# A decoder block on one core: the mixers' steps cut at each hand-over with TensorE, weight splits ordered two blocks ahead, and gv, gr as 512-column blocks

## The chip, the core and the metric

The kernel runs on one core of a Trainium2 chip, as one launch. The metric is the device time of a run in microseconds. The engines are TensorE (PE; its weight loads are PEld), VectorE (DVE), ScalarE (ACT), GpSimd (POOL) and SyncE (SP), whose queue issues the DMAs.

## The reference, cut to what matters

One block over 2048 positions of width 1024, in fp32:

```python
mod = (silu(c) @ w_ada + b_ada)                    # shift, scale, gate for each half
h = rms_norm(x, norm1_g) * (1 + sc1) + sh1
gq, gk, gv, gr, glr, aq, ak, av = split(h @ w_in)  # 256, 256, 512, 512, 16, 512, 512, 512 columns
log_a = log_sigmoid(glr @ gla_w_gate + gla_b_gate) / 16
y_gla = rms_norm(gated_linear_attention(gq, gk, gv, log_a)) * silu(gr)    # 4 heads
y_att = dilated_attention(rms_norm(aq), rms_norm(ak), av)   # 8 heads, windows (128,1), (512,4), (2048,16), merged by their denominators
x = x + g1 * (concat(y_gla, y_att) @ w_out)
h = rms_norm(x, norm2_g) * (1 + sc2) + sh2
u_gate, u_val = split(causal_conv3(h @ w_up))      # 2 x 2816 columns
x = x + g2 * ((silu(u_gate) * u_val) @ w_down)
```

## The kernel before, in words

The 2048 positions go in four chunks c of T = 512. Each large product is three fp32r matmuls for every 128 rows k of the inner dimension (mm3, L233): both operands are split into a high part (hi, rounded to fp32r) and the rest (lo), and hi x hi, hi x lo and lo x hi are added up in one accumulator bank. Weights come as blocks of 512 KB: a DMA into wraw (2 buffers), a cast on ScalarE to whi (L223) and a subtraction on VectorE, or POOL, to wlo (L224), 3 buffers each (wslot, L214). Large products use 4 accumulator banks (psg, given by pg()), the small ones 4 others (psa).

The stages of a chunk:

- proj(c) multiplies the normalised chunk by w_in. Channel blocks (chan: q, k of the attention with their norm, gq, gk) have the weights as stationary operand and 512 positions as columns. Token blocks (tok(b), L393; b = 0, 1 is gv, 2, 3 gr, 4, 5 av; b = 0 holds the 16 columns of glr too) have 128 positions as stationary operand and 256 (272) weight columns. Their results go to DRAM (gv, rg, v and so on). In tok(3) a hook makes the next chunk's normalised pieces hhi, hlo (norm_mod1, L327): eight pieces, one for each k, in 9 buffers.
- mix(c) is the mixer: gla (L465) for two halves of the chunk, then attn (L592) for four pairs of heads. gla makes scores at eight levels (VectorE, ScalarE exponentials, POOL product kh at L525, 32-wide matmuls at L500), then the output and the state. attn makes the scores of three branches (L651 for the 16-dilated one, scores() at L631 for the others) with a running maximum mx, exponentials (soft, L641) with their sums dn, a merging of the branches' denominators in which two small matmuls move values across partitions (with constants x1 at L685 and x4 at L703), scaling by the weights f, transposes (turn, L722) and the products with v (L746, L751). Their results y go to DRAM.
- outproj(c) loads y, splits it and multiplies by w_out; then follow a second norm and ffn(c) with down().

All of these are Python generators; a yield ends a step. beside(a, na, b, nb) takes a step of b and then na/nb steps of a, so the products of one chunk (b) are issued among the mixer steps of another (a): mix(0) beside proj(1) to proj(3), mix(1) beside outproj(0) and ffn(0), and so on. The framework then schedules: each instruction's place in the code is its priority, and on a simulated timeline every engine takes the first that is ready. What comes out is a fixed order for each engine, which the chip follows strictly.

Of the kernel before, what the change touches and what calls it, by code (L numbers as in the profile page):

```python
# [27 lines left out]
FIRST = (0, 1, 2, 3)  # L28

# [99 lines left out]
class K:  # L129
# [102 lines left out]

    def mm3(self, ps, ws, hs, first=True, shared=False):  # L233

        nc = self.nc
        n = len(ws)
        for k in range(n):
            (wh, wl), (hh, hl) = ws[k], hs[k]
            nc.tensor.matmul(ps, wh, hh, start=first and k == 0, stop=False, skip_group_check=shared)  # L239
            nc.tensor.matmul(ps, wh, hl, start=False, stop=False, skip_group_check=shared)  # L240
            nc.tensor.matmul(ps, wl, hh, start=False, stop=k == n - 1, skip_group_check=shared)  # L241
# [97 lines left out]
    def proj(self, c, hs, hook=None, done=()):  # L339
# [45 lines left out]
        def glaqk(b):  # L385
            ps = done[b] if b in done else chan(A["w_ch"][b])
# [6 lines left out]
        def tok(b):  # L393
            if b == 0:
                w = self.wblock(A["w_tok0"][0], 4, 272) + self.wblock(A["w_tok0"][1], 4, 272)
            else:
                w = self.wblock(A["w_tok"][b - 1, 0], 4, 256) + self.wblock(A["w_tok"][b - 1, 1], 4, 256)
            pss = []
# [8 lines left out]
            if b == 3 and hook:  # L407
                hook()
            for s2 in range(2):
                st = stage()  # L410
                if b:
                    ps = pss[s2]
                for s in range(2 if b == 0 else 0):
                    ps = self.pg()
                    tk = slice((2 * s2 + s) * P, (2 * s2 + s + 1) * P)
                    self.mm3(ps[:, 0:272], [(h[:, tk], l[:, tk]) for h, l in hs], w)
                    nc.scalar.copy(st[:, s * 256:(s + 1) * 256], ps[:, 0:256])
                    nc.scalar.copy(gl[:, 2 * s2 + s], ps[:, 256:272])
                v = lambda t: t.rearrange("p (s n) -> p s n", s=2)
                if b // 2 == 1:  # L420
                    nc.scalar.activation(st, ps, AF.Tanh, scale=0.5)
                    nc.vector.scalar_tensor_tensor(st, st, 1.0, ps, op0=ALU.add, op1=ALU.mult)  # L422
# [17 lines left out]
        if done:  # L440
            yield from chain(glaqk(0), glaqk(1), glaqk(2), glaqk(3), tok(0), qk(0), qk(1), tok(1), qk(2), qk(3), tok(4), qk(4), tok(5), qk(5), qk(6), tok(2), qk(7), tok(3))
        else:
            yield from chain(tok(0), qk(0), qk(1), tok(1), qk(2), glaqk(0), qk(3), tok(4), qk(4), glaqk(1), qk(5), tok(5), qk(6), glaqk(2), qk(7), tok(2), glaqk(3), tok(3))
# [21 lines left out]
    def gla(self, c, a):  # L465
# [47 lines left out]
        scores(gk, gq, 0)  # L513
        yield
        for s in (32, 16, 8, 4, 2, 1, 64):
# [10 lines left out]
            scores(kh, qh, s)  # L526
            yield
# [9 lines left out]
        nc.gpsimd.tensor_tensor(el, gk, el, op=ALU.mult)  # L537
        ps = self.pa()
# [8 lines left out]
        for s in range(2):  # L547
            sb = self.sb[s]
            part = lambda t, j: t[j:j + 32].rearrange("p e (h s) q -> p e h s q", s=2)[:, :, :, s]
            full = lambda j, q: sb[j:j + 32, :, q:q + 32].rearrange("p (h e) q -> p e h q", e=2)  # L550
            for j in range(0, P, 32):
                nc.vector.tensor_copy(full(j, j), part(av, j))
            for j in (0, 64):
                nc.gpsimd.tensor_copy(full(j, j + 32), part(a32, j))
            for e in range(2):
                nc.scalar.copy(sb[0:64, e::2, 64:P], off[e][0:64, 0:256].rearrange("p (h s q) -> p h s q", h=2, s=2)[:, :, s])
# [20 lines left out]
        nc.scalar.activation(ss, ss, AF.Exp, scale=-0.5)  # L577
        for s in range(2):
            o = os[s]
            y = t2("pt", 5)  # L580
            for hd in range(4):
                nc.vector.scalar_tensor_tensor(y[:, hd * P:(hd + 1) * P], o[:, hd * P:(hd + 1) * P], ss[:, s, hd:hd + 1], rg[:, s * T + hd * P:s * T + (hd + 1) * P], op0=ALU.mult, op1=ALU.mult)
            ps = self.pa()
            for hd in range(4):
                nc.tensor.transpose(ps[:, hd * P:(hd + 1) * P], y[:, hd * P:(hd + 1) * P], self.C("id"))
# [3 lines left out]
            yield  # L589


    def attn(self, c, hp):  # L592
# [22 lines left out]
        S = []  # L615
# [28 lines left out]
        slp = self.C("slp")[:, 24 * hp:24 * hp + 24].rearrange("p (a g i) -> p a g i", a=2, g=3)  # L644
        for hh in range(2):
# [19 lines left out]
        yield  # L665
# [3 lines left out]
        for hh in range(2):  # L669
            nc.vector.scalar_tensor_tensor(nm[:, hh], mx[:, hh], -1.0, slp[:, hh], op0=ALU.mult, op1=ALU.mult)  # L670
# [12 lines left out]
        nc.vector.tensor_tensor(xm, mv[:, :, None, :].to_broadcast(x4), self.C("s1")[:, None, :, None].to_broadcast(x4), op=ALU.mult)  # L683
        ps = self.pa()
# [16 lines left out]
        nc.vector.tensor_tensor(xm, f[:, :, 2][:, :, None, :].to_broadcast(x2), self.C("s4")[:, None, :, None].to_broadcast(x2), op=ALU.mult)  # L701
        ps = self.pa()
# [4 lines left out]
        yield  # L707
        for hh in range(2):
            _, s4, sn = S[hh]
            for i in range(4):  # L710
                z = 0 if c else P
                nc.vector.tensor_scalar(s4[:, i, z:], s4[:, i, z:], f[:, hh, 1, i:i + 1], None, op0=ALU.mult)
# [279 lines left out]
```

## Time and profile before

| | |
|---|---|
| median of 3 runs | 2737.36 us (2737.02 to 2742.2) |
| the profiled execution | 2739.4 us, span 2737.6 us |
| granted TensorE clock, mean | 0.978 |
| DMA packets moved | 405.19 MB, 148 GB/s |
| span | TensorE busy 96%, VectorE 69%, ScalarE 46%, POOL 19% |

The page gives for each engine its busy time, share of the span and instructions. Matmuls overlap in the pipeline, so the time that one adds is read from start to start of neighbours and not from its duration. "Granted clock" is the share of full speed at which TensorE was allowed to run. In a row of waits, `PE psa L685 <- DVE xm L683` is a matmul of line 685 that waited for VectorE's line 683.

### The profile page before, as it was taken

The numbers are of one execution on the slowest core, as the hardware profiler recorded it, in microseconds if no ns is written. First come the engines' busy times: TensorE is split into PE (matmuls) and PEld (weight loads), VectorE is DVE, ScalarE is ACT, GpSimd is POOL, SyncE is SP. The second block draws the span as 40 slices with busy tenths as digits, with TensorE's granted clock in tenths as the row PEclk, the third lists the DMA queues.
The fourth block names the chain that finished last, engine by engine and source line by source line (L and its number), as shares of the span: only waits on it lengthen the run. The fifth ranks groups of instructions, "written<-read, shape, count | busy, mean of one in ns | idle before, by whom it ended". The sixth has DMA issues, their size and how long they took to land.

```text
span 2737.6 us, 48297 instructions
## 1 busy us (share of the span) xinstructions
PE 2622.8 (96%) x18920; PEld 2172.7 (79%) x18920; DVE 1889.6 (69%) x3740; ACT 1265.5 (46%) x2606; POOL 518.8 (19%) x324
## 2 busy tenths in 40 slices
PE   5989999999979999999999999999999999999999
PEld 4978888888858887778777888887777788788887
DVE  8777575555567776667987677778877667575655
ACT  3555456465435444443544444435444444343332
POOL 1233242222222211100230111013111100011110
PEclk9999999999979999999999999999999999999999
DMA  7877454554632333336434444544443435333232
GB/s 276 289 260 243 145 186 154 195 173 147 197 113 93 99 123 122 106 122 232 137 97 124 130 136 126 169 168 128 130 129 113 140 122 187 125 100 100 93 100 93
DMA packets 196230, 405.19 MB, mean 148 GB/s; under 512 B 19474, under 2 KB 78627, under 8 KB 194723
## 3 DMA queue, kind: packets, MB, share of 16 engines
q1 hardware_dynamic: 196002, 402.11, 45.1%
q8 instruction: 149, 2.44, 0.4%
q14 instruction: 79, 0.64, 0.1%
HBM read 339.12 MB, written 62.91 MB: 147 GB/s over the span
## 4 chain that ended last, share of the span: by engine, by line
PE 66%; DVE 14%; ACT 9%; DMA 7%; issue 3%; SPq 1%; POOL 0%; DVEq 0%; ACTq 0%; POOLq 0%
PE psg L239 19%; PE psg L241 19%; PE psg L240 19%; DMA wada<-in_w_ada_dram 3%; ACT big L641 3%; DVE wlo L224 2%; PE psa L722 2%; PE psa L631 2%; PE psa L751 2%; ACT whi L223 1%; ACT s L641 1%; DVE big L637 1%; DMA sq<-in_xT_dram 1%; DVE wada L281 1%; DVE y L819 1%
## 5 line engine op out<-in xcount | busy, mean ns | idle before, releaser
L239 PE MATMUL psg<-hhi,whi 128*128 128x512 f32 x2040 | 818.5, 403 | 21.9 <-ACT hhi L333 10.4
L241 PE MATMUL psg<-hhi,wlo 128*128 128x512 f32 x2040 | 808.8, 397 | 10.6 <-DVE wlo L224 10.5
L240 PE MATMUL psg<-hlo,whi 128*128 128x512 f32 x2040 | 808.4, 397 | 7.2 <-DVE hlo L335 7.1
L223 ACT CAST whi<-wraw 128x1024 fp32r<-128x1024 f32 x391 | 408.6, 1049 | 573.9 <-PE psg L240 400.5
L224 DVE TENSOR_TENSOR wlo<-wraw,whi 128x1024 fp32r<-128x1024 f32 (+1 forms) x300 | 393.8, 1313 | 188.4 <-ACT whi L223 177.1
L224 POOL TENSOR_TENSOR wlo<-wraw,whi 128x1024 fp32r<-128x1024 f32 x91 | 225.6, 2479 | 1392.7 <-ACT whi L223 1169.3
L239 PEld LDWEIGHTS psg<-hhi,whi 128*128 128x128 f32 x2040 | 390.1, 191 | 115.9 <-ACT hhi L333 13.9
L241 PEld LDWEIGHTS psg<-hhi,wlo 128*128 128x128 f32 x2040 | 389.4, 191 | 96.2 <-DVE wlo L224 13.9
L240 PEld LDWEIGHTS psg<-hlo,whi 128*128 128x128 f32 x2040 | 390.3, 191 | 89.5 <-DVE hlo L335 10.8
L239 PE MATMUL psg<-ghi,whi 128*128 128x512 f32 x704 | 279.3, 397 | 0.0
L240 PE MATMUL psg<-glo,whi 128*128 128x512 f32 x704 | 277.1, 394 | 0.0
L241 PE MATMUL psg<-ghi,wlo 128*128 128x512 f32 x704 | 274.4, 391 | 0.0
L863 DVE SCALAR_TENSOR_TENSOR x<-psg,mod,x 128x512 f32<-128x512 f32 x192 | 143.0, 748 | 159.2 <-PE psg L241 154.8
L239 PE MATMUL psg<-whi,hhi 128*128 128x256 f32 (+1 forms) x768 | 222.5, 292 | 7.9 <-DVE stg L422 3.9
L241 PE MATMUL psg<-whi,hlo 128*128 128x256 f32 (+1 forms) x768 | 222.1, 292 | 5.6 <-DVE hlo L335 5.6
L240 PE MATMUL psg<-wlo,hhi 128*128 128x256 f32 (+1 forms) x768 | 221.4, 290 | 0.4 <-DVE wlo L224 0.4
L819 DVE SCALAR_TENSOR_TENSOR y<-psg,conv_w_sb,y 128x511 f32<-128x511 f32 x176 | 130.9, 744 | 94.1 <-ACT y L818 93.5
L239 PEld LDWEIGHTS psg<-whi,hhi 128*128 128x128 f32 x768 | 149.8, 196 | 12.4 <-issue 3.7
L239 PEld LDWEIGHTS psg<-ghi,whi 128*128 128x128 f32 x704 | 132.2, 188 | 33.1 <-issue 5.4
L241 PEld LDWEIGHTS psg<-whi,hlo 128*128 128x128 f32 x768 | 149.8, 196 | 8.5 <-DVE hlo L335 6.8
L240 PEld LDWEIGHTS psg<-glo,whi 128*128 128x128 f32 x704 | 132.3, 188 | 28.8 <-issue 3.1
L241 PEld LDWEIGHTS psg<-ghi,wlo 128*128 128x128 f32 x704 | 132.2, 188 | 27.9 <-DVE wlo L224 0.6
(198 smaller groups left out, 3672.9 us busy)
## 6 DMA issues: line engine op xcount, KB each, us to landing
wraw<-in_w_up_dram SPq DMA_DIRECT2D x176, 512.0 KB, 3.4
wraw<-in_w_down_dram SPq DMA_DIRECT2D x88, 512.0 KB, 3.4
wraw<-in_w_ch_dram SPq DMA_DIRECT2D x48, 512.0 KB, 4.0
wada<-in_w_ada_dram SPq DMA_DIRECT2D x40, 512.0 KB, 5.0
wraw<-in_w_tok_dram SPq DMA_DIRECT2D x40, 512.0 KB, 4.0
v<-v SPq DMA_DIRECT2D x68, 256.0 KB, 5.1
wraw<-in_w_out_dram SPq DMA_DIRECT2D x32, 512.0 KB, 4.0
sq<-in_xT_dram SPq DMA_DIRECT2D x48, 256.0 KB, 3.7
```

The source lines that it names most:

```text
L223: nc.scalar.copy(hi[:, :n], raw[:, :n])
L224: (nc.gpsimd if pool else nc.vector).tensor_tensor(lo[:, :n], raw[:, :n], hi[:, :n].bitcast(F32), op=ALU.subtract)
L239: nc.tensor.matmul(ps, wh, hh, start=first and k == 0, stop=False, skip_group_check=shared)
L240: nc.tensor.matmul(ps, wh, hl, start=False, stop=False, skip_group_check=shared)
L241: nc.tensor.matmul(ps, wl, hh, start=False, stop=k == n - 1, skip_group_check=shared)
L281: self.last = nc.vector.tensor_tensor_reduce(raw, raw, self.cond[:, i * n:(i + 1) * n], 0.5, m if i else 0.0, ALU.mult, ALU.add, m)
L631: nc.tensor.matmul(at(i, hh, z), q[H[hh], i * P:(i + 1) * P], key(H[hh], i, z), start=True, stop=True, skip_group_check=True)
L641: nc.scalar.activation(t[:, lo:hi], t[:, lo:hi], AF.Exp, bias=nm[:, hh, g, i:i + 1], scale=2.0 ** -(h + 1), accum_out=dn[:, hh, g, i:i + 1])
L722: nc.tensor.transpose(ps[:n, i * P:(i + 1) * P], part(S[hh], i), self.C("id"))
L751: nc.tensor.matmul(out, lhsT, rhs, start=first[hh], stop=False, skip_group_check=True)
L819: nc.vector.scalar_tensor_tensor(y[:, 1:], ps[:, :T - 1], self.cw[:, 1, b:b + 1], y[:, 1:], op0=ALU.mult, op1=ALU.add)
L863: nc.vector.scalar_tensor_tensor(x1, ps, self.mod[:, 40 + cb:41 + cb], x1, op0=ALU.mult, op1=ALU.add)
```

## The change

1. **Token blocks.** gv and gr are made by wide(b) as four weight blocks of two k each and 512 columns; all four accumulator banks are taken at once, one for each 128 positions, and filled over all eight k. av(b) keeps 256 columns (av and glr: 272). The order of the blocks of proj is now a list: ORDER0 for chunk 0, ORDER for the others (W wide, V av, q attention channels, g gq and gk).
2. **Weights.** plan() lists all weight blocks in the order of use; weights() issues the DMA and the split of the block two places ahead before it gives out the one asked for.
3. **Mixer steps.** In gla the scores of a level are issued in the step after their operands (prep), and the copies into sb come a step ahead of the matmuls that read them. In attn the negated maximum nm and the exponentials are made for each branch by itself (exps), the step ends ahead of the x1 and the x4 matmul, and the scaling of s4 and of sn stands behind each. There are 68 steps in a mixer, 76 before; 26 in a proj, 30 before.
4. The numbers of beside() follow the new step counts.

```diff
+ORDER0 = "g0 g1 g2 g3 V0 q0 q1 W0 q2 q3 V1 q4 q5 q6 q7 W1".split()
+ORDER = "W0 V0 q0 q1 q2 g0 q3 V1 q4 g1 q5 q6 g2 q7 g3 W1".split()
...
+    def weights(self, name, *idx, ahead=2):
+        while len(self.wready) <= self.wpos + ahead and self.wleft:
+            n, i, k, m, pool = self.wleft.pop(0)
+            self.wready.append(((n, i), self.wblock(self.A[n][i], k, m, pool)))
+        key, w = self.wready[self.wpos]
...
+        def wide(b):
+            pss = [self.pg() for _ in range(4)]
+            for j in range(4):
+                w = self.weights("w_tokw", b, j)
+                for i in range(2):
+                    for s in range(4):
+                        h, l = hs[2 * j + i]
+                        tk = slice(s * P, (s + 1) * P)
+                        self.mm3(pss[s], [(h[:, tk], l[:, tk])], w[i:i + 1], i == 0 and j == 0, True)
+                if j < 3:
+                    yield
+            if b == 1 and hook:
+                hook()
+            for s in range(4):
+                st = stage()
+                if b:
+                    nc.scalar.activation(st, pss[s], AF.Tanh, scale=0.5)
+                    nc.vector.scalar_tensor_tensor(st, st, 1.0, pss[s], op0=ALU.add, op1=ALU.mult)
+                    nc.gpsimd.tensor_tensor(st, st, self.gB.rearrange("p a b -> p (a b)"), op=ALU.mult)
+                else:
+                    nc.scalar.copy(st, pss[s])
+                nc.sync.dma_start(D["rg" if b else "gv"][s * P:(s + 1) * P, :], st)
+            yield
...
+        def exps(g, part):
+            nc.vector.scalar_tensor_tensor(nm[:, :, g], mx[:, :, g], -1.0, slp[:, :, g], op0=ALU.mult, op1=ALU.mult)
+            for hh in range(2):
+                for i in range(4):
+                    soft(*part(hh, i))
...
         scores(qf, lambda R, r, z: k4[R, r].rearrange("p w m -> p (w m)")[:, z:], z4, self.C("b4"), s4, 1)
+        exps(0, lambda hh, i: (s16[hh], hh, 0, i, i * nk, (i + 1) * nk))
         yield
         scores(qn, lambda R, b, z: k1[R, b * P + z:b * P + 256], z1, self.C("b1"), sn, 2)
-        yield
+        exps(1, lambda hh, i: (s4[hh][:, i], hh, 1, i, z4(i), 256))
...
-        for hh in range(2):
-            nc.vector.scalar_tensor_tensor(nm[:, hh], mx[:, hh], -1.0, slp[:, hh], op0=ALU.mult, op1=ALU.mult)
-            for i in range(4):
-                soft(s16[hh], hh, 0, i, i * nk, (i + 1) * nk)
...
-            yield
+        yield
+        exps(2, lambda hh, i: (sn[hh][:, i], hh, 2, i, z1(i), 256))
...
         nc.vector.tensor_tensor(xm, mv[:, :, None, :].to_broadcast(x4), self.C("s1")[:, None, :, None].to_broadcast(x4), op=ALU.mult)
+        yield
         ps = self.pa()
         nc.tensor.matmul(ps[:, 0:64], self.C("x1"), xm.rearrange("p a r b -> p (a r b)"), start=True, stop=True)
...
+        for hh in range(2):
+            for i in range(4):
+                z = 0 if c else P
+                nc.vector.tensor_scalar(s4[hh][:, i, z:], s4[hh][:, i, z:], f[:, hh, 1, i:i + 1], None, op0=ALU.mult)
+        turn(nk, 0, lambda t, i: t[0][:, i * nk:(i + 1) * nk], lambda t: t[0][:nk].rearrange("p (r n) -> p r n", n=P))
+        yield
         ps = self.pa()
         nc.tensor.matmul(ps[:, 0:32], self.C("x4"), xm.rearrange("p a b r -> p (a b r)"), start=True, stop=True)
...
-        for _ in range(30):
+        for _ in range(27):
             next(gemm)
-        beside(self.mix(0), 72, gemm, 92)
-        beside(self.mix(1), 76, chain(self.outproj(0), self.ffn(0)), 86)
+        beside(self.mix(0), 68, gemm, 76)
+        beside(self.mix(1), 68, chain(self.outproj(0), self.ffn(0)), 86)
```

What the change makes of the order, at three places. First ScalarE in the first attention pair of chunk 1 (s_ is the 16-dilated branch's tile, big those of the other two; L818, L825, L829 before and L888, L895, L899 now are work of ffn). Before:

```order
L829 ACTIVATE th<-y_10419 128x512
L641 ACTIVATE s_10228,md<-s_10228,nm 128x64 x4
L641 ACTIVATE big,md<-big,nm 128x256 x8
L641 ACTIVATE s_10229,md<-s_10229,nm 128x64 x2
L818 ACTIVATE y_10475<-psg,conv_b_sb,conv_w_sb 128x512
L641 ACTIVATE s_10229,md<-s_10229,nm 128x64 x2
L641 ACTIVATE big,md<-big,nm 128x256 x8
L818 ACTIVATE y_10535<-psg,conv_b_sb,conv_w_sb 128x512
L825 COPY halo<-psg 128x2
L223 CAST whi<-wraw 128x1024 x2
```

Now:

```order
L895 COPY halo<-psg 128x2
L709 ACTIVATE s_9620,md<-s_9620,nm 128x64 x4
L709 ACTIVATE s_9621,md<-s_9621,nm 128x64 x4
L226 CAST whi<-wraw 128x1024
L888 ACTIVATE y_9707<-psg,conv_b_sb,conv_w_sb 128x512
L895 COPY halo<-psg 128x2
L899 ACTIVATE th<-y_9707 128x512
L226 CAST whi<-wraw 128x1024
L709 ACTIVATE big,md<-big,nm 128x256 x16
L226 CAST whi<-wraw 128x1024 x2
L171 COPY s_9620<-psa 64x512
```

The 24 exponentials stood in one run with one ffn instruction in it, and the casts of weights behind; now the eight of the 16-dilated branch stand ahead, with two casts and ffn work between them and the other sixteen.

Second TensorE at the edge from chunk 0 to chunk 1 of the projections, with buffer numbers (before, hhi_1825, 1832, 1839 are the fourth to sixth normalised piece and psg_1887 and 1914 two banks; now hhi_1626, 1633, 1640 are the third to fifth, hhi_1612 the first, psg_1690 and 1691 two banks). Before:

```order
L240 MATMUL psg_1914<-wlo_1877,hhi_1825 128x272
L241 MATMUL psg_1914<-whi_1876,hlo_1827 128x272
L239 MATMUL psg_1887<-whi_1882,hhi_1832 128x272
L240 MATMUL psg_1887<-wlo_1883,hhi_1832 128x272
L239 MATMUL psg_1914<-whi_1882,hhi_1832 128x272
L240 MATMUL psg_1914<-wlo_1883,hhi_1832 128x272
L483 MATMUL psa_2011<-consts_sb_458,s16_2003 128x128 x4
L241 MATMUL psg_1887<-whi_1882,hlo_1834 128x272
L239 MATMUL psg_1887<-whi_1882,hhi_1839 128x272
```

Now:

```order
L290 MATMUL psg_1690<-whi_1581,hlo_1628 128x512
L288 MATMUL psg_1690<-whi_1581,hhi_1633 128x512
L289 MATMUL psg_1690<-wlo_1582,hhi_1633 128x512
L290 MATMUL psg_1690<-whi_1581,hlo_1635 128x512
L288 MATMUL psg_1690<-whi_1696,hhi_1640 128x512
L288 MATMUL psg_1691<-whi_1546,hhi_1612 128x512
L289 MATMUL psg_1691<-wlo_1547,hhi_1612 128x512
L290 MATMUL psg_1691<-whi_1546,hlo_1614 128x512
L288 MATMUL psg_1691<-whi_1546,hhi_1619 128x512
```

The first token block of chunk 1 used all pieces in its first two banks; now one bank gets four pieces and one matmul of the fifth, and then the other banks follow with the first pieces again.

Third TensorE at the end of mix(0) (L766, now L836, transposes the last output of its last attention pair; L483, now L540, and L500, now L557, belong to gla of chunk 1; rows with 128x512 are large matmuls). Before:

```order
L751 MATMUL psa<-big,v_7621 64x8x16 x14
L766 MATMUL psa<-consts_sb,pt 128x128 x4
L483 MATMUL psa<-consts_sb,s_8244 128x128 x4
L500 MATMUL psa<-kt 32x32 x32
L500 MATMUL psa<-pt 32x32 x63
L239 MATMUL psg<-hhi,whi 128x512 x3
L500 MATMUL psa<-pt 32x32 x10
L240 MATMUL psg<-hlo,whi 128x512
```

Now:

```order
L821 MATMUL psa<-big,v_6588 64x8x16 x14
L289 MATMUL psg<-wlo,hhi 128x512
L290 MATMUL psg<-whi,hlo 128x512
L288 MATMUL psg<-whi,hhi 128x512
L836 MATMUL psa<-consts_sb,pt 128x128 x4
L289 MATMUL psg<-wlo,hhi 128x512
L290 MATMUL psg<-whi,hlo 128x512
L288 MATMUL psg<-whi,hhi 128x512
L289 MATMUL psg<-wlo,hhi 128x512
L290 MATMUL psg<-whi,hlo 128x512
```

Before, no large matmul stood between that transpose and the ones that read the last piece of y. Now five of the gr block and 42 of the output projection come ahead of L540, and 21 more behind it.

More of the change, by code (lines that the diff above doesn't have):

```diff
@@ L438, in tok @@
                 yield
[L440 to L443, printed above, removed]
+        ops = dict(W=wide, V=av, g=glaqk, q=qk)
+        yield from chain(*(ops[o[0]](int(o[1])) for o in (ORDER if c else ORDER0)))
     def gate(self, c, gl):
@@ L537, in gla @@
         nc.gpsimd.tensor_tensor(el, gk, el, op=ALU.mult)
+        for s in range(2):
+            sb = self.sb[s]
+            part = lambda t, j: t[j:j + 32].rearrange("p e (h s) q -> p e h s q", s=2)[:, :, :, s]
+            full = lambda j, q: sb[j:j + 32, :, q:q + 32].rearrange("p (h e) q -> p e h q", e=2)
+            for j in range(0, P, 32):
+                nc.vector.tensor_copy(full(j, j), part(av, j))
+            for j in (0, 64):
+                nc.gpsimd.tensor_copy(full(j, j + 32), part(a32, j))
+            for e in range(2):
+                nc.scalar.copy(sb[0:64, e::2, 64:P], off[e][0:64, 0:256].rearrange("p (h s q) -> p h s q", h=2, s=2)[:, :, s])
+        yield
         ps = self.pa()
@@ L548, in gla @@
             sb = self.sb[s]
[L549 to L556, printed above, removed]
             o = self.pa()
@@ L644, in attn, with turn @@
         slp = self.C("slp")[:, 24 * hp:24 * hp + 24].rearrange("p (a g i) -> p a g i", a=2, g=3)
+        def turn(n, b0, part, to):
+            for hh in range(2):
+                ps = self.pa()
+                for i in range(b0, 4):
+                    nc.tensor.transpose(ps[:n, i * P:(i + 1) * P], part(S[hh], i), self.C("id"))
+                self.copy(to(S[hh]), ps[:n, b0 * P:].rearrange("p (r n) -> p r n", n=P))
+        def exps(g, part):
[3 more added lines that the diff above has]
+                    soft(*part(hh, i))
         for hh in range(2):
@@ L706, in attn @@
         nc.vector.tensor_reduce(f[:, :, 2], xm, AX.X, ALU.add)
-        yield
         for hh in range(2):
[L709 to L712, printed above, removed]
             for i in range(4):
                 z = 0 if (c or i) else P
-                nc.vector.tensor_scalar(sn[:, i, z:], sn[:, i, z:], f[:, hh, 2, i:i + 1], None, op0=ALU.mult)
-        def turn(n, b0, part, to):
-            for hh in range(2):
-                ps = self.pa()
-                for i in range(b0, 4):
-                    nc.tensor.transpose(ps[:n, i * P:(i + 1) * P], part(S[hh], i), self.C("id"))
-                self.copy(to(S[hh]), ps[:n, b0 * P:].rearrange("p (r n) -> p r n", n=P))
+                nc.vector.tensor_scalar(sn[hh][:, i, z:], sn[hh][:, i, z:], f[:, hh, 2, i:i + 1], None, op0=ALU.mult)
         def weigh(out, g):
@@ L959, in layout @@
     w = w_in[0]
-    tokcols = np.concatenate([w[:, 512:1536], w[:, 2576:3088]], 1)
+    wide = lambda a: a.reshape(4, 2, P, T).transpose(0, 2, 1, 3).reshape(4, P, 2 * T)
     half = lambda a, n: pack_blocks(a, n).reshape(-1, P, 2, 4 * n).transpose(0, 2, 1, 3)
```

141 lines of the change are left out of this document (81 added, 60 removed).

## The prediction

> **What bounds the kernel now.** I read the page's head first, then the windows by stage, then the waits of TensorE, then the timelines of the places where it waits.
>
> ```profile
> PE 2622.8 (96%) x18920; PEld 2172.7 (79%) x18920; DVE 1889.6 (69%) x3740; ACT 1265.5 (46%) x2606; POOL 518.8 (19%) x324
> PEclk9999999999979999999999999999999999999999
> ```
>
> TensorE is busy 2622.8 of 2737.6 us, so 114.8 us of idle time can go without taking work from it. The clock row says that some of the busy time runs slowed. The windows tell where both are. Columns: length, busy time of each engine, granted clock (the third number from the end).
>
> ```profile
> 0.00:62.00 62.00, 32.14 (x100) 21.69 (x100) 52.33 (x105) 21.90 (x30) 10.96 (x10) 0.94 0.77 273
> 130.00:280.00 150.00, 134.21 (x1186) 118.35 (x1185) 113.93 (x172) 81.70 (x131) 55.83 (x44) 0.93 0.76 245
> 280.00:400.00 120.00, 115.86 (x1133) 104.45 (x1133) 80.42 (x114) 60.46 (x121) 45.07 (x36) 0.96 0.48 159
> 550.00:595.00 45.00, 41.65 (x289) 38.11 (x288) 26.96 (x55) 31.86 (x71) 6.91 (x6) 1.00 0.45 147
> 748.00:800.00 52.00, 38.83 (x458) 30.45 (x455) 31.90 (x44) 18.16 (x32) 12.54 (x11) 0.80 0.47 149
> 800.00:824.00 24.00, 17.16 (x183) 12.19 (x183) 18.52 (x31) 12.01 (x20) 4.83 (x3) 0.64 0.21 68
> 1058.00:1078.00 20.00, 16.07 (x58) 12.14 (x57) 14.86 (x29) 11.44 (x36) 5.03 (x2) 0.83 0.16 54
> 1138.00:1158.00 20.00, 15.85 (x56) 11.86 (x55) 14.09 (x28) 10.20 (x28) 5.14 (x2) 0.83 0.22 79
> 1218.00:1238.00 20.00, 15.12 (x56) 11.36 (x55) 15.19 (x33) 9.41 (x26) 4.81 (x2) 0.83 0.25 79
> 1480.00:1500.00 20.00, 15.83 (x54) 11.97 (x53) 14.33 (x28) 12.86 (x40) 5.17 (x2) 0.74 0.16 52
> 1700.00:2080.00 380.00, 374.39 (x2898) 302.67 (x2897) 289.64 (x582) 175.17 (x389) 66.20 (x39) 1.00 0.45 145
> 2080.00:2102.00 22.00, 18.17 (x68) 13.88 (x67) 14.93 (x32) 15.04 (x48) 4.87 (x2) 0.84 0.14 51
> 2355.00:2395.00 40.00, 35.86 (x139) 27.77 (x139) 27.23 (x40) 18.16 (x23) 6.39 (x3) 0.91 0.43 145
> ```
>
> Idle is length less PE busy; the most that the clock can have cost is length times (1 - clock). Idle inside a slowed stretch costs nothing twice, so from that bound up to half the idle may have to be taken off.
>
> - Group A, five attention stretches (1058, 1138, 1218, 1480, 2080): idle 3.93 + 4.15 + 4.88 + 4.17 + 3.83 = 21.0; clock 3.4 + 3.4 + 3.4 + 5.2 + 3.5 = 18.9 at most, 8.4 at least. I take 15: 36 in all.
> - Group B, end of the first mixer (748 to 800): idle 13.2; clock 10.4 at most, 3.8 at least. The slowed part holds most of the idle, so I take 5: 18.
> - Group C, projections (130 to 400, 550 to 595): idle 15.8 + 4.1 + 3.4 = 23.3; clock 10.5 + 4.8 = 15.3 at most, 5.3 at least; I take 11: 34.
> - Left alone by the edits: the start (29.9 idle), 800 to 824 (6.8, the second norm of chunk 0) and 2355 to 2395 (4.1, the same norm of chunk 3). The rest, 16 us, is scattered (5.6 of it between 1700 and 2080, at full clock).
>
> ```profile
> PE psg L239 <- ACT hhi L333: 13.4, 7, 5.2
> PE psg L241 <- DVE wlo L224: 10.5, 5, 2.6
> PE psa L685 <- DVE xm L683: 10.5, 8, 2.5
> PE psa L500 <- POOL pt L525: 8.1, 3, 3.7
> PE psa L363 <- POOL sqr L357: 6.8, 5, 2.4
> PE psg L239 <- DVE stg L422: 3.9, 2, 2.5
> ```
>
> **The change part by part: attention steps (group A).** One of the five places, on TensorE, ScalarE and VectorE in turn:
>
> ```profile
> 1063.70 0.39 PE L241 MATMUL psg<-hhi,wlo 128*128 128x512 f32 x1
> 1065.79 0.43 PE L685 MATMUL psa<-xm,consts_sb 128*128 128x64 f32 x2 [1.70 <-DVE xm L683]
> 1069.70 0.80 PE L241 MATMUL psg<-hhi,wlo 128*128 128x512 f32 x1 [2.04 <-DVE wlo L224]
> ```
>
> ```profile
> 1051.92 0.35 ACT L641 ACTIVATE s<-s,nm 128x64 f32<-128x64 f32 x1 [0.27 <-DVE nm L670]
> 1064.40 0.50 ACT L641 ACTIVATE big<-big,nm 128x256 f32<-128x256 f32 x1
> 1064.89 1.98 ACT L223 CAST whi<-wraw 128x1024 fp32r<-128x1024 f32 x2
> ```
>
> ```profile
> 1065.51 0.22 DVE L683 TENSOR_TENSOR xm<-md,consts_sb 128x64 f32<-128x64 f32 x1
> 1066.91 2.74 DVE L224 TENSOR_TENSOR wlo<-wraw,whi 128x1024 fp32r<-128x1024 f32 x1 [0.16 <-ACT whi L223]
> ```
>
> All 24 exponentials wait for one nm (L670), which needs the maxima of all three branches. They fill ScalarE from 1051.9 to 1064.9. TensorE reaches the x1 matmul at 1064, the last sum is not there, and it stands 1.70 us. Behind the exponentials two weight casts were held up, and the subtraction that follows lasted 2.74 us, so it stands 2.04 us more for wlo. Now each branch has its nm, the eight exponentials of the first branch leave a whole step earlier, and only sixteen lie together: ScalarE's last clump shrinks by a third, some 4 of 13 us, which is as much as both waits together (3.7). The casts are also asked for earlier. What is late next: the x4 matmul and the transposes of s4 behind eight scalings on VectorE; in chunk 1's four pairs 35 to 50 large matmuls stand between x1 and x4 in the new order, 33 to 62 before, 8 us or more at the spacing below. I take back 30 of 36; ends 0 and 36.
>
> **End of the first mixer (group B).**
>
> ```profile
> 750.16 0.66 PE L766 MATMUL psa<-consts_sb,pt 128*128 128x128 f32 x4
> 768.35 1.65 PE L239 MATMUL psg<-hhi,whi 128*128 128x512 f32 x3 [3.85 <-ACT hhi L787]
> ```
>
> From the last transpose of mix(0) to the first use of its y by the output projection pass 18.2 us (VectorE, store, load, cast), in which TensorE has only score matmuls of the next mixer, each waiting for POOL (8.1 us). With 68 steps against 76 the mixer ends while the projection still has matmuls: in the new order 68 large ones (5 of gr's block, 63 of the output projection) follow that transpose before the last y is needed. At the spacing worked out below they last 15.4 us. I take back 14 of 18; ends 0 and 18.
>
> **gv, gr as 512-column blocks.** Each of two large matmuls of 256 columns becomes one of 512; 1536 are removed, 768 added. Spacing from start to start:
>
> ```profile
> 2599.66 0.39 PE L239 MATMUL psg<-ghi,whi 128*128 128x512 f32 x1
> 2605.11 0.39 PE L239 MATMUL psg<-ghi,whi 128*128 128x512 f32 x1
> ```
>
> ```profile
> 230.90 0.28 PE L239 MATMUL psg<-whi,hhi 128*128 128x256 f32 x1
> 232.93 0.28 PE L241 MATMUL psg<-whi,hlo 128*128 128x256 f32 x1
> ```
>
> Between the first two rows are 24 steps: 0.227 us each. Between the last two 17: 0.119. So 768 x (2 x 0.119 - 0.227) = 9 us less TensorE work (the durations of 0.39 and 0.28 overlap and would give 131, which is not to be had). The Trainium skill ("TensorE: Matmul & The Clock Gate", Back-to-back issue gap) puts the spacing at N/2.4 + 2.5 ns, 109 and 216 ns: that would be an estimate of 2 us, and a sum 7 us higher. The rows are slower for the short form than the page, so the rows stand.
>
> The blocks take all four accumulator banks:
>
> ```profile
> L223 ACT CAST whi<-wraw 128x1024 fp32r<-128x1024 f32 x391 | 408.6, 1049 | 573.9 <-PE psg L240 400.5
> L224 DVE TENSOR_TENSOR wlo<-wraw,whi 128x1024 fp32r<-128x1024 f32 (+1 forms) x300 | 393.8, 1313 | 188.4 <-ACT whi L223 177.1
> L421 ACT ACTIVATE stg<-psg 128x512 f32<-128x512 f32 x16 | 8.9, 589 | 4.7 <-PE psg L241 4.6
> L422 DVE SCALAR_TENSOR_TENSOR stg<-stg,psg 128x512 f32<-128x512 f32 x16 | 10.7, 681 | 0.5 <-ACT stg L421 0.4
> ```
>
> Emptying gr's four banks one after another is 4 x (0.589 + 0.681) = 5.1 us, gv's by ScalarE alone 4 x 0.589 = 2.4. Banks end 3 x 0.227 = 0.7 us apart and are taken up again in that order, which hides most. Ends: 0, and 4 x (5.1 + 2.4) = 30 over the eight blocks. The nearest row is the wait for L422, 3.9 us in two of the eight gr blocks; I take 1 us a block, 8.
>
> **Other projection edits (group C).** At the first chunk's edge the old order needs the fifth of the eight normalised pieces after 24 matmuls and the last after 82 (2.9 and 9.8 us at 0.119); the new one needs the fifth once after 12 and the sixth only after 60 (2.7 and 13.6 us at 0.227). So the waits for hhi and hlo should fall to one or two. The waits for sqr (6.8) and stg stay in kind. I take half, 17 of 34; ends 0 and 34.
>
> **Splits two blocks ahead.** Three slots of whi and wlo allow no more than that, and ScalarE waits 400.5 us for TensorE to free one: it runs as far ahead already wherever it is free. Costed at nothing beyond group A. The same bytes of weights are loaded. VectorE gets 16 more small instructions and ScalarE one table load, off the path at 69% and 46% busy; POOL loses 16.
>
> **Scattered waits**: 4 of 16; ends 0 and 16.
>
> Sum: 9 + 30 + 14 + 17 + 4 - 8 = 66 off. The profiled execution took 2739.4 us (span 2737.6), 2.0 above the median of the runs: 2739.4 - 66 = 2673. All gains and no bank wait: 9 + 36 + 18 + 34 + 16 = 113, 2626. Half of A and no more beside the 9, with 8 lost: 19, 2720.
>
> **Rivals.**
> 1. Slower: splits stand ahead of the mixer's work. A split is 1.05 us of ScalarE and 1.31 of VectorE, 2.36; a mixer's hand-over that comes late by one stops TensorE, whose order is fixed. There are 4 x 68 = 272 steps. It outweighs the 66 from 28 steps so hit; at one in five (54) it costs 127, and the time is 2673 + 127 = 2800. For it: the same collision the other way round is group A. Against it: the 400.5 us in which ScalarE was ahead as far as it could be.
> 2. The waits only move, from x1 to x4 or to the transposes, and at the chunk's edge from hhi to a bank: then 9 and little of B remain, 2712 to 2730. For it: in chunk 1 x4 and its transposes hang on a chain of a dozen VectorE steps, and no wait for them shows only because 33 large matmuls or more cover it. Against it: that cover stays.
> 3. The clock is not bought back: idle goes, but the slowed stretches have another cause and stay. Of the 66, some 22 are clock (12 of A, 4 of B, 6 of C): 2695. For it: no single wait at 1058 to 1078 is longer than 2.04 us. Against it: the five attention stretches, at 0.74 to 0.84, are just those with about 4 us idle in 20. The Trainium skill (same page, What's actually happening) lets the clock drop only after an idle window of about 3.4 us; by that rule two waits of 1.70 and 2.04 would not drop it, and the 0.83 there speaks against it.
>
> **How the numbers follow.** 0.2% is about what a measurement of this kernel can tell from no change. The forecast (2645 to 2712): 0.72, of which 0.10 is the third rival. Better still: 0.06. Second rival: 0.10. No measurable change, gains and bank waits in balance: 0.04. Slower: 0.08. So faster 0.88, same 0.04, slower 0.08. 2645 to 2712 leaves out 0.28, so the range takes in the near part of the second rival, up to 2720 (the last sum above), and goes down to 2640, a third of the way to 2626.
>
> **What would show it.** Right: the waits of the x1 matmul and for wlo in the attention stretches under 5 us together (21 now), their clock at 1.0; no wait over 2 us for the output projection's first operand; TensorE's matmul count down by 768. Wrong: new waits of turn's transposes or of the x4 matmul, waits for the emptying of a wide block's bank (tanh and product of gr, copy of gv) above 15 us in all, or ScalarE's casts in front of the exponentials with TensorE waiting for either.

## The result and the profile after

| | before | after |
|---|---|---|
| median of 4 runs | 2737.19 us (2735.46 to 2742.2) | 2676.11 us (2675.21 to 2677.89) |
| profiled execution, its span | 2739.4 us, 2737.6 us | 2676.88 us, 2675.1 us |
| granted TensorE clock, mean | 0.978 | 0.989 |

The ratio is 0.9775, with a 95% interval of 0.9758 to 0.9792: 61 us faster. The forecast was 2673. The sum came out; two of its terms did not, and by luck their errors cancelled.

The head of the page after, with the two rows that answer to those shown of before:

```profile
PE 2595.0 (97%) x18152; PEld 2122.1 (79%) x18152; DVE 1891.1 (71%) x3756; ACT 1273.2 (48%) x2607; POOL 512.1 (19%) x308
PEclk9999999999989999999999999999999999999999
```

TensorE has 768 matmuls fewer (18920 before), 27.8 us less busy time and 80.1 us of idle instead of 114.8. The dip of the clock at the end of the first mixer is smaller.

To see where the time went I cut every run at two matmuls that all kernels have: the second norm of chunk 0, where mixer 0 and the projections end, and the same norm of chunk 3. These are the rows of TensorE's timeline, of before and of after:

```profile
807.92 2.04 PE L318 MATMUL psa<-rstd,ones 128*128 128x512 f32 x2 [4.07 <-DVE rstd L316]
2361.18 1.02 PE L318 MATMUL psa<-rstd,ones 128*128 128x512 f32 x2
```

```profile
792.95 1.10 PE L367 MATMUL psa<-rstd,ones 128*128 128x512 f32 x2 [2.90 <-DVE rstd L365]
2298.27 1.02 PE L367 MATMUL psa<-rstd,ones 128*128 128x512 f32 x2
```

Stage I (up to the first) went from 807.9 to 793.0, stage II (between them; mixers 1 to 3 beside outproj and ffn) from 1553.3 to 1505.3, stage III from 376.4 to 376.8. So 15.0 us came from stage I and 47.9 from stage II. The windows of these stages, before and after (length, busy time of each engine, clock third from the end):

```profile
0.00:808.00 808.00, 736.54 (x6097) 640.08 (x6097) 524.66 (x1000) 421.61 (x828) 229.57 (x176) 0.96 0.61 201
808.00:2361.00 1553.00, 1517.61 (x11220) 1229.55 (x11221) 1130.86 (x2387) 710.63 (x1616) 236.04 (x126) 0.98 0.41 132
```

```profile
0.00:793.00 793.00, 727.81 (x5265) 595.57 (x5265) 539.02 (x1001) 425.82 (x828) 217.90 (x159) 0.98 0.61 204
793.00:2298.00 1505.00, 1498.16 (x11283) 1223.41 (x11284) 1117.45 (x2402) 714.01 (x1616) 241.17 (x127) 1.00 0.43 136
```

In stage II idle fell from 35.4 to 6.8 us (28.6). Busy time fell by 19.5 us, although 64 small score matmuls of gla came into it from stage I: the clock record has 52 us at half clock in this stage before and 14 after. Together that is 48. The waits of TensorE after, down to 2.4 us:

```profile
PE psa L367 <- DVE rstd L365: 17.5, 2, 14.6
PE psg L288 <- ACT hhi L382: 9.0, 4, 5.4
PE psg L289 <- DVE wlo L227: 7.2, 4, 4.8
PE psg L288 <- DVE stg L461: 7.0, 3, 3.9
PE psa L411 <- ACT sqr L405: 5.2, 2, 4.6
PE psg L289 <- DVE hlo L384: 5.0, 4, 1.9
PE psa L412 <- POOL sqr L406: 4.6, 4, 1.9
PE psa L557 <- ACT rstd L369: 2.9, 2, 1.4
PE psg L288 <- ACT hhi L857: 2.7, 1, 2.7
PE psg L288 <- DVE y L890: 2.5, 1, 2.5
PE psg L288 <- ACT stg L464: 2.4, 1, 2.4
```

The x1 matmul (L764 now) is not among them. Of the waits for hhi and hlo, 8.6 and 3.7 us lie in the first 100 us, at the start that the edits leave alone (8.3 and 5.7 before). What is new lies in stage I: wlo, the emptying of gr's and gv's banks (L461, L464) and the wait of L411 for sqr.

### The profile page after: what moved, and what is told of

Same layout as the page of the kernel before. It is cut to its first block, busy times and chain, and to the rows that moved or that the text cites. A ratio compares the mean times of both kernels' runs of the same rounds, so it can differ in the third digit from the quotient of the medians.

```text
span 2675.1 us, 46823 instructions
## 1 busy us (share of the span) xinstructions
PE 2595.0 (97%) x18152; PEld 2122.1 (79%) x18152; DVE 1891.1 (71%) x3756; ACT 1273.2 (48%) x2607; POOL 512.1 (19%) x308
## 4 chain that ended last, share of the span: by engine, by line
PE 77%; DVE 5%; ACT 3%; DMA 2%; issue 1%; POOL 0%; SPq 0%; DVEq 0%; ACTq 0%; POOLq 0%
PE psg L288 22%; PE psg L289 22%; PE psg L290 22%; PE psa L719 2%; PE psa L699 2%; PE psa L821 2%; PE psa L557 1%; DVE wlo L227 1%; ACT whi L226 1%; PE psa L816 1%; PE psa L735 1%; ACT big L709 1%; PE psa L627 0%; PE psa L628 0%; DMA sq<-y 0%
## 5 line engine op out<-in xcount | busy, mean ns | idle before, releaser
L288 PE MATMUL psg<-hhi,whi 128*128 128x512 f32 x2040 | 808.7, 399 | 15.6 <-ACT hhi L382 9.0
L290 PE MATMUL psg<-hhi,wlo 128*128 128x512 f32 x2040 | 803.9, 395 | 0.0
L226 ACT CAST whi<-wraw 128x1024 fp32r<-128x1024 f32 (+1 forms) x391 | 409.6, 1049 | 402.5 <-PE psg L289 307.5
L227 DVE TENSOR_TENSOR wlo<-wraw,whi 128x1024 fp32r<-128x1024 f32 (+1 forms) x300 | 386.1, 1287 | 150.2 <-ACT whi L226 141.4
L288 PE MATMUL psg<-whi,hhi 128*128 128x512 f32 (+2 forms) x512 | 177.5, 353 | 10.5 <-DVE stg L461 7.0
L289 PE MATMUL psg<-wlo,hhi 128*128 128x512 f32 (+2 forms) x512 | 178.7, 349 | 7.2 <-DVE wlo L227 7.2
L290 PE MATMUL psg<-whi,hlo 128*128 128x512 f32 (+2 forms) x512 | 177.3, 349 | 0.0
L709 ACT ACTIVATE big<-big,nm 128x256 f32<-128x256 f32 (+1 forms) x256 | 122.4, 479 | 47.1 <-DVE nm L724 47.1
L581 POOL TENSOR_TENSOR pt<-kt,pt 128x512 f32<-128x512 f32 x56 | 92.4, 1650 | 264.2 <-ACT pt L578 186.5
```

Source lines behind the costliest of these rows:

```text
L226: nc.scalar.copy(hi[:, :n], raw[:, :n])
L227: (nc.gpsimd if pool else nc.vector).tensor_tensor(lo[:, :n], raw[:, :n], hi[:, :n].bitcast(F32), op=ALU.subtract)
L581: nc.gpsimd.tensor_tensor(kh, gk, df, op=ALU.mult)
L709: nc.scalar.activation(t[:, lo:hi], t[:, lo:hi], AF.Exp, bias=nm[:, hh, g, i:i + 1], scale=2.0 ** -(h + 1), accum_out=dn[:, hh, g, i:i + 1])
```

## The experiments

Stage I, II and the whole, by one profile each; the ratio is from the timed runs, against runs of before on the same chip (medians 2733.45, 2732.62 and 2731.47 us in the three groups). Before was profiled only on the first chip, where its runs were 4 to 6 us longer, and a profile is one run. So the stage columns tell where time went, to a few us, and the ratio tells how much: wide_alone, for one, is 9 us slower than before by the profiles and 18 by the runs. Of a longer edit the fences show only some lines.

| kernel | ratio (95%) | stage I | stage II |
|---|---|---|---|
| before | 1 | 807.9 | 1553.3 |
| steps_alone | 0.9843 (0.9829 to 0.9856) | 804.4 | 1505.4 |
| ahead_alone | 0.9867 (0.9853 to 0.988) | 804.3 | 1516.2 |
| wide_alone | 1.0067 (1.0053 to 1.008) | 817.5 | 1552.7 |
| undo_steps | 0.9867 (0.9852 to 0.9882) | 797.9 | 1515.3 |
| undo_wide | 0.9794 (0.9776 to 0.9811) | 791.5 | 1505.3 |
| undo_balance | 0.9844 (0.9827 to 0.986) | 807.7 | 1506.7 |
| undo_ahead | 0.9797 (0.9782 to 0.9812) | 791.2 | 1505.1 |
| exps_alone | 0.9819 (0.9802 to 0.9836) | 802.7 | 1503.3 |
| exps_balance | 0.9799 (0.9786 to 0.9812) | 795.3 | 1504.7 |
| steps_clump | 0.9962 (0.9949 to 0.9974) | 803.9 | 1537.1 |
| pool_split | 0.9895 (0.9881 to 0.9908) | 818.5 | 1503.5 |
| balance_76 | 0.9771 (0.9755 to 0.9787) | 785.9 | 1505.1 |
| after | 0.9775 (0.9758 to 0.9792) | 793.0 | 1505.3 |

**One part at a time.** steps_alone has the new gla and attn in the kernel before, with mix(0) ending against the GEMM steps where it ended before:

```diff
-        beside(self.mix(0), 72, gemm, 92)
+        beside(self.mix(0), 64.4, gemm, 92)
```

> The kernel before with the new mixer steps alone (68 steps; token blocks and the moment of the splits as before, and the balance of mix(0) scaled from 72/92 to 64.4/92, so that again some five steps are left over when the projections end). Theory: the attention steps carry group A, so the waits of the x1 matmul and for wlo there go, and some of the scattered waits with them: 36 to 41 us off, 2696 to 2701, and group B stays. Rival, that the splits two blocks ahead carry the wlo half of group A: only the x1 half goes, 15 to 20 us off, 2717 to 2722.

2690.08 us, 43 off: below what either theory gave. In stage II neither x1 nor wlo waits any more.

ahead_alone has plan() and weights() with before's blocks and mixers.

```diff
-            w = self.wblock(src, KD, m)
+            w = self.weights("w_ch", b)
```

> The kernel before with the weight splits ordered two blocks ahead, and nothing else. Theory: three slots already let ScalarE run that far, so nothing that can be measured: 2733 to 2740. Rival, that the splits carry the wlo waits in attention: those five waits and their slowed clock go, 15 to 20 us off, 2717 to 2722.

2696.38 us, 37 off, beyond the rival too: "costed at nothing" falls for this edit alone. Its timelines at the first attention pair of chunk 1 (ScalarE, VectorE, TensorE):

```profile
1062.31 0.20 ACT L696 ACTIVATION_READ_ACCUMULATOR big<-big,nm 128x1 f32 x1
```

```profile
1062.54 0.23 DVE L738 TENSOR_TENSOR xm<-md,consts_sb 128x64 f32<-128x64 f32 x1 [0.21 <-ACT big L696]
```

```profile
1066.33 0.40 PE L294 MATMUL psg<-hhi,whi 128*128 128x512 f32 x1
1066.56 0.33 PE L740 MATMUL psa<-xm,consts_sb 128*128 128x64 f32 x2
```

The clump of exponentials is as long as ever, and xm comes right behind it; but TensorE reaches x1 only 4.0 us after that, behind large matmuls. Counted in the traces, 47 to 64 large matmuls stand between the first exponential and x1 in the twelve pairs of chunks 1 to 3 before, 71 to 85 with the splits ahead (58 in one pair). The step is about one weight block, 24 matmuls. From the last exponential to x1 there was none in eight of the twelve pairs before, and there are 10 to 22 now. In the order of before the next block's split stood behind the clump, so TensorE had nothing to put ahead of x1.

wide_alone has wide(), av() and ORDER with before's mixers and a split at each use.

```diff
-                w = self.wblock(A["w_tok"][b - 1, 0], 4, 256) + self.wblock(A["w_tok"][b - 1, 1], 4, 256)
+            pss = [self.pg() for _ in range(4)]
```

> The kernel before with gv and gr as 512-column blocks in the new order of blocks, splits at the moment of use, mixer steps as before, and mix(0)'s balance such that again some six steps are left over. Theory: 9 us of matmul time less, and in the projections as many new waits as go: 9 off, 2728 (2722 to 2734). Rival, the prediction's group C with its bank waits: 9 + 17 - 8 = 18 off, 2719.

2751.0 us, 18 slower; both theories fall. Three of TensorE's waits; before there were 3.9 us in two for L422, 0.4 in one for wlo of the token blocks and 0.5 in two for sqr from ScalarE:

```profile
PE psg L288 <- DVE stg L461: 17.6, 4, 4.8
PE psg L289 <- DVE wlo L227: 6.6, 4, 5.0
PE psa L411 <- ACT sqr L405: 4.8, 1, 4.8
```

Each of gr's four blocks keeps the next bank back for 4.4 us on average, not much less than the 5.1 us that the prediction counts for emptying four banks one after another.

**One part undone.** undo_steps has before's gla and attn; mix(0) gets its 76 steps of 76.

```diff
-        beside(self.mix(0), 68, gemm, 76)
+        beside(self.mix(0), 76, gemm, 76)
```

> The changed kernel with the old mixer steps (76; balance 76/76, so that the mixer still ends with the projections). Theory: group A and the scattered waits come back, 36 to 41 us more than the changed kernel, 2712 to 2717. Rival, that the splits ahead already mend half of group A by themselves: 15 to 20 more, 2691 to 2696.

2697.5 us, next to the rival's range; the theory falls. Stage II is that of ahead_alone, 38 off in its profile (which is the shortest of four runs, 2690.07), so without the steps the splits do what they do alone.

undo_wide is the changed kernel with before's token blocks and their order:

```diff
-        def wide(b):
+        def tok(b):
...
-        beside(self.mix(0), 68, gemm, 76)
+        beside(self.mix(0), 68, gemm, 89)
```

> The changed kernel with the 256-column token blocks and before's order of projection steps put back; the new steps, the splits two ahead and the later end of GEMM against mix(0) (68 to 89 steps) stay. Theory now, from the first four runs: alone the 512-column blocks made the kernel 18 us slower (2733.5 to 2751.0), because the four evacuations of rg's banks take PE's next bank away (17.6 us in 4 waits for stg, line 461) and two more waits of 5 us came (wlo at 107 us, sqr at 179 us); in the changed kernel the same waits come to 9.4 + 4.9 + 4.8 = 19 us against 9 us of shorter matmul spacing, so without them 2655 to 2665, faster than the changed kernel (2672 on this chip's scale, 0.9775 of 2733.5). Rival (the prediction's sum: -9 for the columns, +8 for the banks): 2671 to 2675, no difference.

2674.52 us, where the changed kernel's ratio would give 2671; the intervals overlap. The theory that I had formed from wide_alone (12 us and more to be had) falls: beside the other parts the 512-column blocks are worth nothing either way that these runs can tell.

This run tests more than the columns: it also puts back the order of blocks on which the prediction's group C rests. By the prediction's terms it should be 9 + 17 - 8 = 18 us slower than the changed kernel; it is 3.5 us slower, within what the intervals hide. Its waits between 100 and 600 us:

```profile
PE psg L296 <- DVE hlo L390: 7.1, 4, 3.2
PE psa L418 <- POOL sqr L412: 5.4, 5, 2.3
PE psa L417 <- ACT sqr L411: 3.1, 2, 2.7
PE psg L294 <- DVE stg L477: 1.1, 1, 1.1
PE psg L294 <- ACT hhi L388: 0.8, 1, 0.8
```

The waits for hhi and hlo are back, 7.9 us, and those for banks and wlo are all but gone: the new order exchanges the ones for the others.

undo_balance:

```diff
-        beside(self.mix(0), 68, gemm, 76)
+        beside(self.mix(0), 62, gemm, 76)
```

> The changed kernel with mix(0) ending where it ended before against the GEMM steps (62 to 76 instead of 68 to 76), so that the last transposes of the mixer come when no large matmul is left beside them. Theory: the 14 us that the prediction booked for the end of mix(0) come from this balance alone: 2684 to 2690, with the idle time of PE in 700 to 840 us back at 18 to 20 us (9.5 in the changed kernel) and the granted clock there at 0.88 (0.94). Rival: the shorter steps alone keep PE fed there, 2670 to 2675.

2690.98 us, 1 us over the theory's range, and stage I back at 807.7. The place itself, in before and in this run:

```profile
748.00:808.00 60.00, 42.76 (x536) 33.48 (x532) 38.91 (x51) 21.07 (x38) 15.58 (x12) 0.81 0.45 140
```

```profile
748.00:808.00 60.00, 44.80 (x553) 35.87 (x552) 37.96 (x50) 20.87 (x36) 13.86 (x11) 0.84 0.41 138
```

15.2 us idle, 17.2 before: the finer steps alone do not feed TensorE there. What does is that with 68 for 62 the mixer runs faster against the projections, so that it ends while they still have large matmuls.

undo_ahead:

```diff
-    def weights(self, name, *idx, ahead=2):
+    def weights(self, name, *idx, ahead=0):
...
-            w = self.weights(f"w_av{b}", 0) + self.weights(f"w_av{b}", 1, ahead=1)
+            w = self.weights(f"w_av{b}", 0) + self.weights(f"w_av{b}", 1, ahead=0)
```

> The changed kernel with every weight block split when it is used, as before (the plan asked for no block ahead). The prediction costed the splits two ahead at nothing: 2671 to 2675. After the run of the splits alone (37 us faster than before, with no wait for x1's operand left) that can hold only if the new steps have already taken what the splits take: in the attention stretches the steps alone left 1.9 us of idle in 1000 to 1800 us, the changed kernel 3.6. Theory now: nothing lost there, but the 512-column blocks lose more without splits ahead (18 us alone, about 10 with splits ahead), so 2680 to 2688. Rival: the two add, 2694 or more.

2676.99 us, 2 above what the prediction would give and 3 below the theory, with an interval that takes in both and overlaps that of the changed kernel. Both stages are those of the changed kernel to 2 us. Beside the new steps the splits ahead bring nothing that can be told.

**The cause in stage II.** exps_alone puts nothing but the exponentials into the kernel before:

```diff
+        exps(0, lambda hh, i: (s16[hh], hh, 0, i, i * nk, (i + 1) * nk))
         yield
...
+        exps(1, lambda hh, i: (s4[hh][:, i], hh, 1, i, z4(i), 256))
...
-            nc.vector.scalar_tensor_tensor(nm[:, hh], mx[:, hh], -1.0, slp[:, hh], op0=ALU.mult, op1=ALU.mult)
...
+            if hh == 0:
+                exps(2, lambda hh, i: (sn[hh][:, i], hh, 2, i, z1(i), 256))
```

> The kernel before with one edit: each branch's nm and its eight exponentials directly behind that branch's scores, all hand-overs, blocks and splits as before. The prediction's cause for the waits of the attention stretches was the clump of 24 exponentials behind one nm: then 2701 to 2708, x1's waits (10.5 us in 8) under 3 us and the granted clock 1.0 between 1000 and 1800 us. Rival: the place of x1 in PE's queue decides, with which the steps or the splits ahead push it behind more matmuls; the exponentials then end earlier but x1 is issued earlier as well, and the time is 2720 to 2733.

2682.55 us, 50 off: more than expected, and stage II is 1503.3, that of the whole change to 2 us. There the waits of x1 and for wlo, 10.5 us each before, are gone.

```profile
803.00:2306.00 1503.00, 1494.78 (x11221) 1221.61 (x11220) 1122.66 (x2399) 712.55 (x1616) 237.57 (x127) 1.00 0.42 136
```

Between the last exponential and x1 now stand 14 to 51 large matmuls in those twelve pairs. steps_clump is the counter-test, steps_alone with before's clump:

```diff
-        exps(2, lambda hh, i: (sn[hh][:, i], hh, 2, i, z1(i), 256))
+        for hh in range(2):
+            nc.vector.scalar_tensor_tensor(nm[:, hh], mx[:, hh], -1.0, slp[:, hh], op0=ALU.mult, op1=ALU.mult)
```

> The kernel steps_alone with one thing put back: the 24 exponentials of a head pair stand again in one clump behind nm, twelve for each head; all the other new hand-over steps stay. Theory: the exponentials by branch carry the gain of the steps (exps_alone took 50 us, steps_alone 43), so 2720 to 2733, with waits for xm and wlo back and the granted clock at 0.97 to 0.99 in 1000 to 1800 us. Rival: the finer steps themselves feed PE: 2690 to 2700.

2721.83 us. The clump gives 32 of the 43 us back; beside it the other steps are worth about 10. But x1 is not the only place where it costs. TensorE's longest waits in stage II, without that of the norm:

```profile
PE psg L294 <- ACT hhi L860: 8.7, 1, 8.7
PE psa L767 <- DVE xm L764: 4.4, 3, 2.7
PE psg L296 <- DVE wlo L231: 3.4, 3, 1.9
```

```profile
804.00:2341.00 1537.00, 1508.99 (x11284) 1225.43 (x11285) 1116.98 (x2391) 713.18 (x1619) 244.91 (x128) 0.99 0.41 133
1260.00:1300.00 40.00, 31.34 (x224) 24.38 (x223) 20.99 (x27) 12.13 (x23) 7.93 (x7) 0.87 0.55 185
```

The waits of x1 and for wlo come back in part, 7.8 us against 21. The 8.7 us are the output projection of chunk 1 waiting for the end of mix(1), a wait that neither before nor steps_alone has; with the slowed clock beside it that place costs up to 14 of the 32 us. So exps_alone, and not this run, is the evidence for x1.

**What is left in stage I.** exps_balance tries two small edits for the whole:

```diff
-        beside(self.mix(0), 72, gemm, 92)
+        beside(self.mix(0), 82.3, gemm, 92)
```

> The kernel before with two small edits: each branch's exponentials directly behind its scores (which alone took off 50 us) and mix(0) ending later against the GEMM steps (82.3 to 92 instead of 72 to 92), with before's steps, blocks and splits. Theory: the 50 us of the attention stretches and the 20 us that undo_balance lost at the end of mix(0) are different places, so nearly all of the change comes from these two: 2660 to 2668, at or below the changed kernel (2671 on this chip's scale). Rival: before's longer steps leave PE waiting at the end of mix(0) with matmuls at hand or not, so the balance brings at most 5 us: 2676 to 2683.

2677.11 us, in the rival's range. The two small edits reach the whole change as far as these runs can tell (0.9799 and 0.9775, the intervals overlap), though not by the balance as I had thought: against exps_alone the intervals overlap too, and by the profiles stage I gives 7.4 us, not 15. ("Ending later" above means that the large matmuls end later against the mixer.) Where the rest stayed is seen in two windows, 130 to 400 us of exps_alone, then the same window and the end of the mixer in exps_balance:

```profile
130.00:400.00 270.00, 250.48 (x2339) 222.99 (x2338) 197.37 (x287) 143.21 (x253) 103.60 (x80) 0.96 0.63 209
```

```profile
130.00:400.00 270.00, 244.12 (x2314) 215.83 (x2313) 197.61 (x298) 143.84 (x264) 102.47 (x80) 0.96 0.62 205
740.00:795.00 55.00, 51.20 (x565) 41.45 (x564) 44.78 (x56) 23.38 (x42) 20.01 (x16) 0.98 0.48 165
```

The end is filled (3.8 us idle), but the mixer, pushed forward, costs 6.4 us more idle among the projections, with new waits of 4.2 us for a score's operand (L524) and 3.5 for an output of gla (L582).

pool_split:

```diff
-                    yield from (("w_tokw", (b, j), 2, T, False) for j in range(4))
+                    yield from (("w_tokw", (b, j), 2, T, True) for j in range(4))
```

> The changed kernel with the subtraction of the 512-column token blocks on GpSimd (2.46 us each in its trace) instead of VectorE (1.33 us). Theory: in the projection stage the split stands in VectorE's queue behind reductions of the modulation, which wait for their own load (24.5 us in 16 waits between 90 and 400 us); on GpSimd, busy 19%, the waits for wlo (7.2 us in 4) fall under 3: 2664 to 2669 on this chip's scale of 2671. Rival: GpSimd's longer subtraction comes later itself or keeps sqr and nwt back behind it, and the time is 2671 to 2680.

2703.9 us: both theories fall. TensorE's waits between 100 and 600 us:

```profile
PE psg L288 <- DVE stg L461: 13.4, 3, 7.7
PE psa L557 <- DVE pt L580: 7.9, 1, 7.9
PE psa L412 <- POOL sqr L406: 7.5, 4, 3.1
PE psg L289 <- POOL wlo L227: 3.6, 3, 1.7
PE psg L290 <- DVE wlo L227: 3.1, 1, 3.1
```

The waits for these blocks' wlo fall to 3.6 us, but one of 3.1 us for a wlo that VectorE still makes comes in, and those for gr's banks, for an operand of gla (7.9 in one) and for GpSimd's own sqr grow by more. So this move does not relieve the stage; what bounds it is left open.

balance_76:

```diff
-        beside(self.mix(0), 68, gemm, 76)
+        beside(self.mix(0), 76, gemm, 76)
```

> The changed kernel with 76 steps of mix(0) for 76 of GEMM instead of 68, so that still more large matmuls come after the mixer's last transposes. Theory: of the 9.5 us of idle and the clock of 0.94 that the changed kernel keeps in 700 to 840 us another part goes: 2664 to 2669. Rival: what is left there are waits of the mixer's own chain, which another balance only moves; the mixer then runs further ahead into the stage in which the projections wait: 2671 to 2680.

2667.95 us, in the theory's range, ratio 0.9771, the lowest of all, and stage I 7 us shorter in its profile than in the changed kernel; the interval does not tell it from the changed kernel. Between 700 and 840 us idle is 8.3 us, 9.5 in the changed kernel, and the clock 0.95, 0.94 there.

## Why the prediction was right, and where it was not

- **Group A, 30 of 36, and scattered, 4.** The cause was right: exps_alone takes nothing but the clump apart, and the waits go. It was not the whole cause: ahead_alone leaves the clump, puts matmuls ahead of x1, and x1's waits go too. The size was too low: stage II gave 48. In the five places the clock stood at 0.50 for 6.83, 6.83, 6.83, 10.24 and 6.83 us by the trace's record, up to 18.8 us lost, where I had taken 15 from rounded windows; the clock and the idle came back nearly in full, and 7.6 us of scattered idle in the stage went as well. The check named for it holds: no wait for x1, none of wlo in the attention stretches, clock 1.00.
- **Group B, 14 of 18.** undo_balance puts it at 14.8 by the profiles (807.70 less 792.95 us of stage I) and at 20 by the runs (2690.98 against 2671), whose intervals leave some 6 us either way. The mechanism, large matmuls behind the last transpose, is shown; but in exps_balance a like shift gives half as much with before's steps, 7.4 us by the profiles and no more than the intervals hide by the runs. The first operand of outproj still waits 2.7 us, over the 2 that I had set.
- **Group C, 17 of 34.** Wrong. Stage I fell by 15.0, and the balance accounts for all of it. undo_wide, without group C's order, is not slower by anything near 17. The waits for hhi and hlo did go: between 100 and 600 us they were 8.6 us, and none is left. In their place stand wlo (6.8, none before) and the banks (9.4, 3.9 before); the waits for sqr stay (7.9, 7.3 before), now 4.6 of them in one for L411. TensorE's idle in 130 to 400 us is 21.5 us, 19.9 before:

```profile
130.00:400.00 270.00, 248.48 (x1996) 203.53 (x1995) 202.53 (x287) 141.62 (x250) 105.58 (x74) 0.96 0.62 205
```

  The step that failed is "I take half": I counted which waits the new order removes and not which come next. wlo was no wait there before, and I had no term for it.
- **512-column blocks, -9, and their banks, +8.** Two rows of a wide block after:

```profile
399.81 0.40 PE L288 MATMUL psg<-whi,hhi 128*128 128x512 f32 x1
403.68 0.39 PE L290 MATMUL psg<-whi,hlo 128*128 128x512 f32 x1
```

  Between them are 17 steps of 0.228 us, as forecast, so the 9 us of TensorE work are there, and 9.4 us of bank waits fit the 8. The net of -1 fits undo_wide's nothing only because group C, which that run undoes too, came to nothing. And it holds in company only: alone the blocks cost 18 us, with 17.6 us of bank waits, inside the ends of 0 and 30 that I had set.
- **Splits ahead, at nothing.** Right in the sum as far as undo_ahead can tell, wrong in the reason. "It runs as far ahead already wherever it is free" fits the 400.5 us of waiting over the whole kernel and is false at the clump, where it counted. Alone the edit takes off 37 us where the exponentials alone take off 50; beside the new steps it takes off nothing that can be told.
- **The rivals.** Splits ahead of the mixer's work (2800): no such wait; alone they gain. Waits only moved (2712 to 2730): true of stage I's group C, not of x1 or turn, and x4 waits 0.3 us once. Clock not bought back (2695): the mean clock went from 0.978 to 0.989.

So the total was right because group C came 17 too high and group A with the scattered waits 14 too low.

## What to carry over

Look at how many independent large matmuls the order places between an engine's last hand-over and the small matmul that needs it; where there are none, start the producer earlier (here each branch's exponentials as soon as its scores are there) or have one more block ready, and do not pay for both. Cost a rebuilt stage by what becomes late next, not by the waits that the edit names. An edit that gains nothing beside others may be a gain or a loss of about 1% alone: test the parts both ways.

## What the runs showed of the hardware

Short waits of TensorE, none as long as a clock period of 3.41 us, halve its clock afterwards. Windows of the kernel before around the x1 matmul at 1065.8 us, cut at the clock record's own periods:

```profile
1061.60:1065.00 3.40, 2.49 (x11) 1.71 (x10) 1.50 (x3) 3.40 (x14) 0.00 (x0) 1.00 0.00 0
1065.00:1068.40 3.40, 1.69 (x6) 0.82 (x6) 3.20 (x6) 2.60 (x4) 2.40 (x1) 1.00 0.00 0
1068.40:1075.20 6.80, 5.50 (x13) 4.34 (x14) 6.00 (x17) 1.84 (x4) 0.91 (x2) 0.50 0.44 154
```

Neither 3.4 us period is idle throughout: TensorE is busy for 2.49 us of the one and 1.69 of the other, and the next 6.8 us run at 0.50. In all traces here the slowed stretches within the span last a multiple of 3.41 us. Laying this grid over the matmul rows of all fourteen traces (whose ends are modelled, and some rows are missing) gives how full a period has to be: after full-clock periods with TensorE busy for less than half, the clock fell 125 times in 129; between 50% and 60% it fell in 32 of 76; above 60% in 7 of more than 10,000. The second period alone, with 1.69 of its 3.40 us busy, is such a case. So here 3.7 us of waits cost up to 3.4 us more, which is why stage II gave 48 us for 28.6 of idle. The Trainium skill ("TensorE: Matmul & The Clock Gate", What's actually happening) has the half clock and a window of 3413 ns, and these agree; it lets the clock fall after an idle window, and in these traces a half-busy one was enough.
